# Queries and keys of three retention heads by seven products of halves instead of eight, with a larger ring for accumulating DMAs

## The chip, the cores and the metric

The kernel runs on one core of a Trainium2 chip. The metric is the device time of one execution in microseconds (us). Each value of a run is the time of one execution; the median of several is compared.

## The reference

Two residual layers over x of 512 tokens by 1024 features, then a final RMS norm. The first layer (latent attention and pooling) is not touched by the change, except for where one of its tiles lives. The second is a retention layer with 4 heads, 256 query and key features and 512 value features per head:

```python
h = rms_norm(x, norm_g)
proj = h @ w_in                                   # 1024 -> 1024 q | 1024 k | 2048 v | 2048 gate
q, k, v, gate = jnp.split(proj, [RET_QK, 2 * RET_QK, 2 * RET_QK + RET_V], axis=-1)
q = apply_rope(q.reshape(B_, T, 4, 256), cos_r, sin_r)
k = apply_rope(k.reshape(B_, T, 4, 256), cos_r, sin_r) * 256 ** -0.5
# o = sum of a forward and a backward retention: scores q k^T times a decay by distance, times v
...
o = (o - mean(o)) * rsqrt(var(o) + eps) * gn_g    # per head
y = (o * silu(gate)) @ w_out
return x + y
```

where `rope` rotates the first 128 features of a head against the second 128: (x1 cos - x2 sin, x2 cos + x1 sin).

## The kernel before

All arithmetic is float32 carried as a pair of fast-mode numbers: `split` writes a high part by a cast on ScalarE (ACT) and the rest by a subtraction on VectorE (DVE). A product of two such pairs is three matmuls on TensorE (PE): high by high, high by low, low by high (`mm3`). A weight tile of 128 x 1024 goes the same way: it is loaded into a buffer `raw` (4 of them) by a DMA from SyncE's queue (SP), then cast to `wH` (4) and subtracted into `wL` (3). Sums stand in PSUM banks of 128 x 512: four called `mm`, two `sc`, two `tr`.

The code is written in one order; a scheduler that knows the program's dependencies sets the order in which each engine's instructions stand, and the engines keep that order. So an instruction that waits holds back everything behind it on its own engine. `pin` keeps an instruction at its place in the written order relative to the others so marked.

The second layer works through the heads one after the other. For head h the stages are:

1. Queries and keys. `qk_gemm` goes through four column blocks of 128 (two of q, two of k), each 8 input blocks times three matmuls over all 512 tokens, and `rope_pair` rotates the results on DVE and splits them. In between PE does the last turn (four transposes) of the head before (`then=pend[2]`).
2. `r_out`: the output projection of the head before, from its turned results `ys`. Its weights are scaled while they are split (`out_weights`). It is written behind the queries and keys so that PE has work while DVE rotates.
3. `r_scores`: keys by queries, scaled and multiplied by the decay on DVE, then split.
4. `vg`: values and gate together by seven products of halves (the 2 x 2 scheme with 7 multiplications): tokens in two halves, input features in even and odd blocks, columns in values and gate. Operand sums of the tokens' side stand ready in `forms`; sums of the weights' side come as a load on SP and an accumulating DMA from GpSimd (POOL) into a tile `tw` or `raw`. The products are called A11, S1, S4, S2, S3, A12 and A22 and go to the sums X, Y and Z. `tt` (two `tw` tiles) is the weight sum that is changed twice on DVE by adding a loaded tile.
5. `r_head_out`: scores by values for each block t of 128 tokens, the product with the gate (DVE, line 871), its squares (ACT, line 872), and the turn of block t - 1 (line 863) after block t's matmuls.

[...] The norm's power -0.5 is a POOL instruction (line 175).

Of the kernel before, what the change touches and what calls it, by code (L numbers as in the profile page):

```python
# [12 lines left out]
F32R = mybir.dt.float32r  # L13
# [3 lines left out]
ALU = mybir.AluOpType  # L17
AX = mybir.AxisListType

P = 128  # L20
T = 512
# [16 lines left out]
def trunk(ctx: ExitStack, tc: tile.TileContext, x, positions, a_norm_g, a_w_in, a_q_norm_g, a_w_uq,  # L38
          a_kv_norm_g, a_w_ukv, a_pool_w, a_pool_scale, a_w_out, r_norm_g, r_w_in, r_decay_fwd,
          r_decay_bwd, r_gn_g, r_w_out, final_norm_g, freqs, edges, out):  # L40
    nc = tc.nc
# [21 lines left out]
    V = nc.vector  # L63
# [4 lines left out]
    def f(ap):  # L68
        return ap.bitcast(F32)
# [53 lines left out]
    lg = C("lg", (P, 8))  # L123
    nlb = C("nlb", (P, 8))
    fsum = C("fsum", (P, 16))
    r2, nr2, r2s = [C(n, (P, 8))[:, 0:4] for n in ("r2", "nr2", "r2s")]
    C("fill", (P, 16))
    w_in = a_w_in[0]
    vrow0 = S("t")[:8, :P]
    nc.scalar.dma_start(vrow0, a_norm_g.rearrange("o (k p) -> (o k) p", p=P))  # L130
# [193 lines left out]
            act(junk[:, 0:256], xt[t][q], AF.Square, accum_out=ssq[:, 4 * t + q:4 * t + q + 1])  # L324
    ss = S("sm", (P, 4))
    V.tensor_reduce(out=ss, in_=ssq.rearrange("p (t q) -> p t q", q=4), axis=AX.X, op=ALU.add)
    R = C("R", (P, T))
    rp = bcast(pow_mhalf(ss, 1.0 / DM))
    nc.scalar.copy(R, rp)

# [334 lines left out]
    def load(tag, first, *more, then=lambda i: i):  # L665
        raw = S(tag, (P, 1024))
        v = raw.rearrange("p (a b) -> p a b", a=2)
        nc.sync.dma_start(v, first)
        for one in more:
            then(G.dma_start(v, one, accum_op=ALU.add))  # L670
# [70 lines left out]
    def qk_gemm(c0, n=2, then=None):  # L741
        pts = []

        def ev(m, pt):
            pts.append(pt)
            if then and m == 0:
                then()

        gemm_T(wr, c0, n, ev, hH, hL)
        return pts  # L750

    def rope_pair(pts, tag):
# [5 lines left out]
        V.tensor_sub(a, a, b)  # L758
        V.tensor_add(c, c, d)
        return split(a, tag), split(c, tag)  # L760

    def vg(h, tt=None):

        tags = dict(X=("mm", "mm"), Z=("mm", "tr"), Y=("mm", "sc"))
# [35 lines left out]

        b11 = [load("raw", src(0, 0, i)) for i in rng]
        if tt is None:
            tt = first_sums(h)
        product("A11", "X", b11, True)
        p1 = [S("t") for _ in rng]
        for p in rng:
# [32 lines left out]
            gs[2 + p] = c  # L839
        return vv, gs  # L840

    def r_scores(q, k, ds, tag):
        ss = []
        for j in range(4):
            tk = slice(j * P, (j + 1) * P)
            pt = PS("sc")
            for i in range(2):
                mm3(pt, k[i][0][:, tk], k[i][1][:, tk], q[i][0], q[i][1], i == 0, i == 1)
            s = S("t")
            V.scalar_tensor_tensor(out=s, in0=pt, scalar=r2s[:, j:j + 1], in1=ds[j], op0=ALU.mult, op1=ALU.mult)  # L850
            ss.append(split(s, tag))
        return ss

# [99 lines left out]
    for h in range(4):  # L953
        A, B = ("qk", "y") if h % 2 == 0 else ("y", "qk")
        if h == 0:
            res = [residual(0), residual(1)]
            next(res[0])
            pq = qk_gemm(0, 1)
            sums_of_halves(0)
            sums_of_halves(1)  # L960
            next(res[0])
            pq += qk_gemm(P, 1)
            pk = qk_gemm(1024, 1)
            sums_of_halves(2)
            sums_of_halves(3)
            next(res[1])
            next(res[1])
        else:
            pq = qk_gemm(h * 256, then=pend[2])
            pk = qk_gemm(1024 + h * 256, 1)  # L970
            rs = out_scale(pend[1])
        q = rope_pair(pq, A)
        k = rope_pair(pk + qk_gemm(1024 + h * 256 + P, 1), A)
        if h == 0:
            V.tensor_add(ss2[:, 0:4], ss2[:, 0:4], ss2[:, 4:8])
            V.tensor_copy(r2, pow_mhalf(ss2[:, 0:4], 1.0 / DM))
# [56 lines left out]
```

## Time and profile before

| what | value |
|---|---|
| median of 3 runs | 794.5 us (793.38 to 794.87) |
| profiled execution, its time | 795.08 us |
| its span, first to last instruction | 793.3 us |
| mean granted clock of TensorE | 0.996 |
| PE busy | 780.8 us, 98% |
| DVE busy | 579.1 us, 73% |
| ACT busy | 403.6 us, 51% |
| POOL busy | 39.1 us, 5% |
| moved by DMA | 80.91 MB |

Busy times are of the profiled execution, and shares are of its span. Matmuls overlap their neighbours, so a matmul's duration is longer than the distance at which matmuls follow one another. Idle time of an engine is put down to the one whose signal ended it. A line such as L871 is a line of the kernel's file; `tw<-...` names the tile that is written, without its number.

### The profile page before, as it was taken

Reading aid. Unit: us, or ns where it says so; the run is one execution under the profiler, and the core shown is the slowest. Engines: PE = TensorE matmul, PEld = TensorE weight load, DVE = VectorE, ACT = ScalarE, POOL = GpSimd, SP = SyncE. Lnnn points to the kernel's source line nnn. Section 1 sums busy time; section 2 is a strip of 40 time slices with the busy share of each in tenths; the row PEclk is TensorE's granted clock in tenths of the full one; section 3 lists DMA queues with packets and bytes.
Section 4 is the critical chain, followed back from the end, with each engine's and each line's share of the span. In section 5 each row is a group of like instructions: output and inputs, shape, how many; then the busy total and the mean of one; then the engine's idle time right before and its main releaser. Section 6 shows DMA issues by size and latency. Waiting matters only on the chain.

```text
span 793.3 us, 9592 instructions
## 1 busy us (share of the span) xinstructions
PE 780.8 (98%) x3546; PEld 642.3 (81%) x3546; DVE 579.1 (73%) x935; ACT 403.6 (51%) x671; POOL 39.1 (5%) x61
## 2 busy tenths in 40 slices
PE   8999999999999999999999999999999999999996
PEld 6888888888888888888877888888888888888885
DVE  4689986768738777899679837788377884767845
ACT  6645346766716754317754833358333583324832
POOL 0000000000000000100010010100101001010003
PEclk9999999999999999999999999999999999999999
DMA  7722233123123312363315732447324473244202
GB/s 240 222 73 80 73 83 91 40 71 100 54 64 93 105 31 78 75 158 112 93 44 131 207 85 80 109 107 198 91 72 117 104 195 84 70 130 95 92 27 107
DMA packets 87832, 80.91 MB, mean 102 GB/s; under 512 B 7868, under 2 KB 67304, under 8 KB 87784
## 3 DMA queue, kind: packets, MB, share of 16 engines
q1 hardware_dynamic: 83128, 71.37, 29.9%
q0 software_dynamic: 4352, 8.39, 6.9%
q8 instruction: 28, 0.46, 0.3%
q10 hardware_dynamic: 304, 0.53, 0.2%
q14 instruction: 20, 0.16, 0.1%
HBM read 76.87 MB, written 2.10 MB: 100 GB/s over the span
## 4 chain that ended last, share of the span: by engine, by line
PE 84%; issue 10%; DVE 3%; POOL 1%; DMA 1%; ACT 0%; SPq 0%; POOLq 0%; DVEq 0%
PE mm L72 19%; PE mm L76 19%; PE mm L75 19%; PE mm L780 4%; PE mm L781 4%; PE mm L778 4%; PE tr L561 2%; PE sc L72 2%; PE sc L75 2%; PE sc L76 2%; PE sc L780 1%; PE sc L781 1%; PE sc L778 1%; PE sc L542 1%; PE sc L543 1%
## 5 line engine op out<-in xcount | busy, mean ns | idle before, releaser
L72 PE MATMUL mm<-hT,wH 128*128 128x512 f32 x352 | 138.8, 394 | 0.0
L75 PE MATMUL mm<-hT,wH 128*128 128x512 f32 x352 | 138.0, 392 | 0.0
L76 PE MATMUL mm<-hT,wL 128*128 128x512 f32 x352 | 137.9, 392 | 0.0
L108 ACT CAST wH<-raw 128x1024 fp32r<-128x1024 f32 (+3 forms) x85 | 74.3, 884 | 114.3 <-PE mm L75 91.2
L109 DVE TENSOR_TENSOR wL<-raw,wH 128x1024 fp32r<-128x1024 f32 (+3 forms) x85 | 85.6, 1012 | 13.1 <-issue 4.7
L76 PEld LDWEIGHTS mm<-hT,wL 128*128 128x128 f32 x352 | 66.5, 189 | 13.9
L75 PEld LDWEIGHTS mm<-hT,wH 128*128 128x128 f32 x352 | 66.5, 189 | 13.6
L72 PEld LDWEIGHTS mm<-hT,wH 128*128 128x128 f32 x352 | 66.6, 189 | 13.4
L770 ACT CAST wH<-raw 128x1024 fp32r<-128x1024 f32 x32 | 33.7, 1054 | 50.1 <-PE mm L76 20.2
L771 DVE TENSOR_TENSOR wL<-raw,wH 128x1024 fp32r<-128x1024 f32 x32 | 38.9, 1222 | 10.3 <-issue 7.1
L770 ACT CAST wH<-tw 128x1024 fp32r<-128x1024 f32 x24 | 25.1, 1047 | 41.0 <-PE mm L76 26.3
L890 ACT ACTIVATE wH<-raw,cols 128x512 fp32r<-128x512 f32 x32 | 21.4, 717 | 44.1 <-issue 33.1
L911 DVE SCALAR_TENSOR_TENSOR xT<-mm,sm,xT 128x512 f32<-128x512 f32 (+1 forms) x33 | 24.2, 733 | 25.1 <-PE mm L76 25.0
L75 PE MATMUL mm<-y,wH 128*128 128x512 f32 x96 | 37.2, 390 | 0.0
L76 PE MATMUL mm<-y,wL 128*128 128x512 f32 x96 | 37.2, 389 | 0.0
L72 PE MATMUL mm<-y,wH 128*128 128x512 f32 x96 | 37.2, 391 | 0.0
L771 DVE TENSOR_TENSOR wL<-tw,wH 128x1024 fp32r<-128x1024 f32 x24 | 29.3, 1222 | 2.8 <-PE tr L780 1.0
L781 PE MATMUL mm<-wH,hT 128*128 128x512 f32 x80 | 31.1, 389 | 0.0
L780 PE MATMUL mm<-wL,hT 128*128 128x512 f32 x80 | 31.1, 389 | 0.0
L778 PE MATMUL mm<-wH,hT 128*128 128x512 f32 x80 | 31.0, 389 | 0.0
L871 DVE TENSOR_TENSOR l<-mm,l 128x512 f32<-128x512 f32 x16 | 11.1, 692 | 23.8 <-PE mm L76 23.8
L490 DVE TENSOR_TENSOR xT<-mm,xT 128x512 f32<-128x512 f32 x24 | 16.5, 690 | 15.0 <-PE mm L76 14.8
(355 smaller groups left out, 1896.5 us busy)
## 6 DMA issues: line engine op xcount, KB each, us to landing
raw<-in_r_w_in_dram SPq DMA_DIRECT2D x48, 512.0 KB, 3.7
raw<-in_a_w_in_dram SPq DMA_DIRECT2D x25, 512.0 KB, 4.0
raw<-in_a_w_out_dram SPq DMA_DIRECT2D x16, 512.0 KB, 3.9
raw<-in_r_w_out_dram SPq DMA_DIRECT2D x16, 512.0 KB, 5.5
tw<-in_r_w_in_dram SPq DMA_DIRECT2D x8, 512.0 KB, 3.9
tw<-in_r_w_in_dram POOLq DMA_DIRECT2D x8, 512.0 KB, 6.9
raw<-in_r_w_in_dram POOLq DMA_DIRECT2D x8, 512.0 KB, 6.2
l<-in_x_dram SPq DMA_DIRECT2D x8, 256.0 KB, 5.7
```

Source lines behind the costliest of these rows:

```text
L72: i = mm(pt, lhsT=lH, rhs=rH, start=st, stop=False)
L75: mm(pt, lhsT=lH, rhs=rL, start=False, stop=False)
L76: mm(pt, lhsT=lL, rhs=rH, start=False, stop=sp)
L108: then(nc.scalar.copy(h[:, c], raw[:, c]))
L109: then(V.tensor_sub(l[:, c], raw[:, c], f(h[:, c])))
L770: nc.scalar.copy(wh, ws[i])
L771: V.tensor_sub(wl, ws[i], f(wh))
L778: mm(o, lhsT=lh, rhs=wh[:, c], start=first and i == 0 and k2 == 0, stop=False, skip_group_check=True)
L780: mm(o, lhsT=lh, rhs=wl[:, c], start=False, stop=False, skip_group_check=True)
L781: mm(o, lhsT=ll, rhs=wh[:, c], start=False, stop=last and k2 == 1, skip_group_check=True)
L890: act(wh[:, c], raw[:, c], AF.Copy, scale=g)
L911: V.scalar_tensor_tensor(out=a, in0=pt[:, :T // n], scalar=rs[:, t:t + 1], in1=a, op0=ALU.mult, op1=ALU.add)
```

## The change

For heads 1 to 3 stage 1 becomes `qk_halves`, the same scheme of seven products as in `vg`, with q's and k's columns as the two column halves. One product has the weights as the fixed side (128 x 128 each) and a half of the tokens, 256 columns, as the moving side: two column blocks times four input blocks times three matmuls. X, Y and Z take three of the four `mm` banks. The results come out as halves of tokens (k of the first half, k of the second, q of the first, q of the second), so each rotation is done by halves, and high and low parts are written by halves. In this scheme one of the two has the wrong sign, and `r_scores` of these heads multiplies with `nr2s` instead of `r2s`. The first weight sum (`tq`, a tile `tw`) is loaded and accumulated behind `vg` of the head before; `t3` is loaded into a `raw` tile and accumulated within the stage. The ring for accumulating DMAs is 2048 instead of 1024. The norm tile R of the first layer takes a buffer of `x2`, which the second layer uses later for operand forms.

```diff
-    r2, nr2, r2s = [C(n, (P, 8))[:, 0:4] for n in ("r2", "nr2", "r2s")]
-    C("fill", (P, 16))
+    r2, nr2, r2s, nr2s = [C(n, (P, 8))[:, 0:4] for n in ("r2", "nr2", "r2s", "nr2s")]
+    C("fill", (P, 8))
...
-    R = C("R", (P, T))
+    R = S("x2")
...
+    def qk_load(tag, h, *srcs):
+        raw = S(tag, (P, 1024))
+        v = raw.rearrange("p (a b) -> p a b", a=4)
+        for i, (r, c) in enumerate(srcs):
+            one = wv[:, r, :, c * 1024 + h * 256:c * 1024 + (h + 1) * 256]
+            if i:
+                pin(G.dma_start(v, one, accum_op=ALU.add))
+            else:
+                nc.sync.dma_start(v, one)
+        return raw
+
+    def qk_halves(h, tag, tt, then):
+        ps_ = {n: PS("mm") for n in "XZY"}
...
+        def product(name, a, w, first):
+            wh, wl = S("wH", (P, 1024), F32R), S("wL", (P, 1024), F32R)
+            nc.scalar.copy(wh, w)
+            V.tensor_sub(wl, w, f(wh))
+            for u in range(2):
+                o = ps_[a][:, u * H2:(u + 1) * H2]
+                for k in range(4):
+                    c = slice(k * 256 + u * P, k * 256 + (u + 1) * P)
+                    rh, rl = forms[k][name]
+                    mm(o, lhsT=wh[:, c], rhs=rh, start=first and u == 0 and k == 0, stop=False,
+                       skip_group_check=True)
+                    mm(o, lhsT=wh[:, c], rhs=rl, start=False, stop=False, skip_group_check=True)
+                    mm(o, lhsT=wl[:, c], rhs=rh, start=False, stop=k == 3, skip_group_check=True)
...
+        def rope(n, half, c):
+            ts = slice(half * H2, (half + 1) * H2)
+            v = c.rearrange("p (u t) -> p u t", u=2)
+            m1, m2 = S("t"), S("t")
+            for m, tab in ((m1, cosr), (m2, sinr)):
+                V.tensor_mul(m.rearrange("p (u t) -> p u t", u=2), v,
+                             tab[:, ts].unsqueeze(1).to_broadcast([P, 2, H2]))
+            o = S("t")
+            V.tensor_sub(o[:, :H2], m1[:, :H2], m2[:, H2:])
+            V.tensor_add(o[:, H2:], m2[:, :H2], m1[:, H2:])
+            for u in range(2):
+                hh, ll = outs[n][u]
+                us = slice(u * H2, (u + 1) * H2)
+                nc.scalar.copy(hh[:, ts], o[:, us])
+                V.tensor_sub(ll[:, ts], o[:, us], f(hh[:, ts]))
+
+        b11 = load("raw", (0, 0))
+        product("A11", "X", b11, True)
+        p1 = S("t")
+        nc.scalar.copy(p1, X)
+        then()
+        b22 = load("raw", (1, 1))
+        product("S1", "Z", tt, True)
+        v = S("t")
+        V.tensor_add(v, Z, p1)
+        t3 = load("raw", (0, 1), (1, 1))
+        V.tensor_add(tt, tt, b22)
+        product("S4", "Z", b22, False)
+        b21 = load("raw", (1, 0))
+        product("S2", "Y", tt, True)
+        u2 = S("t")
+        V.tensor_add(u2, Y, p1)
+        V.tensor_add(u2, Z, u2)
+        rope("k", 0, u2)
+        V.tensor_add(tt, tt, b21)
+        product("S3", "Y", t3, False)
+        V.tensor_add(v, Y, v)
+        rope("k", 1, v)
+        product("A12", "X", b21, False)
+        rope("q", 0, X)
+        product("A22", "Y", tt, False)
+        V.tensor_add(p1, Y, p1)
+        rope("q", 1, p1)
+        return outs["q"], outs["k"]
...
         else:
-            pq = qk_gemm(h * 256, then=pend[2])
-            pk = qk_gemm(1024 + h * 256, 1)
             rs = out_scale(pend[1])
-        q = rope_pair(pq, A)
-        k = rope_pair(pk + qk_gemm(1024 + h * 256 + P, 1), A)
+            q, k = qk_halves(h, A, tq, pend[2])
...
+            V.tensor_scalar(out=nr2s, in0=r2, scalar1=-0.0625, scalar2=1.0, op0=ALU.mult, op1=ALU.mult)
...
-        ss = r_scores(q, k, decay(h), B)
+        ss = r_scores(q, k, decay(h), B, r2s if h == 0 else nr2s)
         vv, gs = vg(h, tt0 if h == 0 else None)
+        if h < 3:
+            tq = qk_load("tw", h + 1, (0, 0), (0, 1))
         pend = r_head_out(ss, vv, gs, A)
...
-    nc = _bacc.Bacc("TRN2", target_bir_lowering=False, num_devices=1, dynamic_dma_scratch_size=1024)
+    nc = _bacc.Bacc("TRN2", target_bir_lowering=False, num_devices=1, dynamic_dma_scratch_size=2048)
```

`load` in `qk_halves` is `qk_load` with the head filled in. The order of the instructions moves at three places. Rows of the changed kernel bear its own line numbers: its L784 is the split of a weight tile in `qk_halves`, L919 and L953 are L837 and L871 of before (gate's evacuation, product with the gate), L973 is L891 of before.

The first place is DVE at the end of `vg` and the begin of `r_head_out` (here of head 0). Before:

```order
L109 TENSOR_TENSOR wL_4317<-raw_4314,wH_4316 128x1024
L793 SCALAR_TENSOR_TENSOR V_4145<-t_3999,sm_4141,V_4144 128x512
L109 TENSOR_TENSOR wL_4357<-raw_4354,wH_4356 128x1024
L837 TENSOR_TENSOR l_992_4216<-mm_3920,t_3958 128x512
L109 TENSOR_TENSOR wL_4388<-raw_4385,wH_4387 128x1024
L837 TENSOR_TENSOR l_993_4219<-sc_3921,t_3959 128x512
L871 TENSOR_TENSOR l_986_4180<-mm_4223,l_986_4180 128x512
```

The same place on DVE now:

```order
L784 TENSOR_TENSOR wL_4338<-raw_4335,wH_4337 128x1024
L875 SCALAR_TENSOR_TENSOR V_4147<-t_4001,sm_4143,V_4146 128x512
L784 TENSOR_TENSOR wL_4379<-tw_4224,wH_4378 128x1024
L919 TENSOR_TENSOR l_993_4218<-mm_3922,t_3960 128x512
L919 TENSOR_TENSOR l_994_4221<-sc_3923,t_3961 128x512
L825 TENSOR_TENSOR tw_4224<-tw_4224,raw_4376 128x1024
L784 TENSOR_TENSOR wL_4413<-raw_4376,wH_4412 128x1024
L953 TENSOR_TENSOR l_987_4182<-mm_4228,l_987_4182 128x512
```

The second weight split there now reads the accumulated tile `tw`, and the sum `tw += b22` and the split of `b22` stand ahead of the first product with the gate.

The second place is POOL in the same stretch. Before:

```order
L670 DMA tw_4697<-in_r_w_in_dram 128x2x512
L670 DMA tw_4700<-in_r_w_in_dram 128x2x512
L175 TENSOR_TENSOR sm_4418<-sm_4416,mhalf 128x4
L670 DMA raw_4779<-in_r_w_in_dram 128x2x512
L670 DMA raw_4782<-in_r_w_in_dram 128x2x512
```

POOL now:

```order
L768 DMA tw_4224<-in_r_w_in_dram 128x4x256
L175 TENSOR_TENSOR sm_4321<-sm_4319,mhalf 128x4
L768 DMA raw_4408<-in_r_w_in_dram 128x4x256
L670 DMA tw_4813<-in_r_w_in_dram 128x2x512
L670 DMA tw_4816<-in_r_w_in_dram 128x2x512
```

The accumulations of the seven products for q and k stand on both sides of the norm's power, and those for the gate stage come behind them.

The third place is the passage from queries and keys to the output projection (`r_out`). On DVE before, the first weight split of the projection (L891) stands right behind the first rotation's sums:

```order
L757 TENSOR_TENSOR t_4424<-mm_4360,l_755_3175 128x512
L758 TENSOR_TENSOR t_4421<-t_4421,t_4422 128x512
L759 TENSOR_TENSOR t_4423<-t_4423,t_4424 128x512
L891 SCALAR_TENSOR_TENSOR wL_4491<-raw_4488,cols,wH_4490 128x512
L82 TENSOR_TENSOR y_4432<-t_4421,y_4431 128x512
```

On DVE now (the last 12 of the rows from S3's evacuation to that split):

```order
L813 TENSOR_TENSOR y_4334<-t_4518,y_4333 128x256
L804 TENSOR_TENSOR t_4554<-mm_4324,l_757_3177 128x512
L840 TENSOR_TENSOR t_4365<-mm_4326,t_4365 128x512
L807 TENSOR_TENSOR t_4557<-t_4553,t_4554 128x256
L808 TENSOR_TENSOR t_4557<-t_4554,t_4553 128x256
L804 TENSOR_TENSOR t_4593<-t_4365,l_756_3176 128x512
L813 TENSOR_TENSOR y_4328<-t_4557,y_4327 128x256
L804 TENSOR_TENSOR t_4594<-t_4365,l_757_3177 128x512
L813 TENSOR_TENSOR y_4330<-t_4557,y_4329 128x256
L807 TENSOR_TENSOR t_4597<-t_4593,t_4594 128x256
L808 TENSOR_TENSOR t_4597<-t_4594,t_4593 128x256
L973 SCALAR_TENSOR_TENSOR wL_4607<-raw_4604,cols,wH_4606 128x512
```

The split of the projection's weights has moved behind all four rotations. On PE before, at the same passage, the matmuls of one bank follow one another:

```order
L76 MATMUL mm_4445<-hT_3544,wL_4442 128x512
L72 MATMUL mm_4504<-wH_4490,qk_4260 128x512
L75 MATMUL mm_4504<-wL_4491,qk_4260 128x512
L76 MATMUL mm_4504<-wH_4490,qk_4261 128x512
L72 MATMUL mm_4504<-wH_4490,qk_4260 128x512
L75 MATMUL mm_4504<-wL_4491,qk_4260 128x512
```

On PE now:

```order
L793 MATMUL mm_4326<-hT_3545,wL_4565 128x256
L72 MATMUL mm_4620<-wH_4606,qk_4265 128x512
L72 MATMUL mm_4634<-wH_4606,qk_4290 128x512
L72 MATMUL mm_4648<-wH_4606,qk_4315 128x512
L72 MATMUL mm_4662<-wH_4606,qk_4372 128x512
L72 MATMUL sc_4751<-y_4327,y_4331 128x512
L72 MATMUL sc_4764<-y_4327,y_4331 128x512
L75 MATMUL mm_4620<-wL_4607,qk_4265 128x512
```

The first high-part matmuls of four banks and of two score tiles have moved ahead of the first matmul that needs the low part `wL`; the two score tiles read the rotated q and k.

More of the change, by code (lines that the diff above doesn't have):

```diff
@@ L760, in rope_pair, with load @@
         return split(a, tag), split(c, tag)
+    def qk_load(tag, h, *srcs):
[10 more added lines that the diff above has]
+        ps_ = {n: PS("mm") for n in "XZY"}
+        def load(tag, *srcs):
+            return qk_load(tag, h, *srcs)
+        def product(name, a, w, first):
[11 more added lines that the diff above has]
+                    mm(o, lhsT=wl[:, c], rhs=rh, start=False, stop=k == 3, skip_group_check=True)
+        X, Y, Z = (ps_[n] for n in "XYZ")
+        outs = {n: [(S(tag, dt=F32R), S(tag, dt=F32R)) for _ in range(2)] for n in "qk"}
+        def rope(n, half, c):
[41 more added lines that the diff above has]
+        return outs["q"], outs["k"]
@@ L802, in vg @@
         if tt is None:
-            tt = first_sums(h)
+            tt = first_sums(h, pin)
         product("A11", "X", b11, True)
@@ L840, in vg, with r_scores @@
         return vv, gs
-    def r_scores(q, k, ds, tag):
+    def r_scores(q, k, ds, tag, rs):
         ss = []
@@ L849, in r_scores @@
             s = S("t")
-            V.scalar_tensor_tensor(out=s, in0=pt, scalar=r2s[:, j:j + 1], in1=ds[j], op0=ALU.mult, op1=ALU.mult)
+            V.scalar_tensor_tensor(out=s, in0=pt, scalar=rs[:, j:j + 1], in1=ds[j], op0=ALU.mult, op1=ALU.mult)
             ss.append(split(s, tag))
@@ L967, in trunk @@
             next(res[1])
-        else:
-            pq = qk_gemm(h * 256, then=pend[2])
-            pk = qk_gemm(1024 + h * 256, 1)
+            q = rope_pair(pq, A)
+            k = rope_pair(pk + qk_gemm(1024 + P, 1), A)
+        else:
             rs = out_scale(pend[1])
-        q = rope_pair(pq, A)
-        k = rope_pair(pk + qk_gemm(1024 + h * 256 + P, 1), A)
+            q, k = qk_halves(h, A, tq, pend[2])
         if h == 0:
```

## The prediction

> **What bounds the kernel now.** I read the page's busy times first, then the stretches of the second layer, then single instructions on each engine around the place of the change.
>
> ```profile
> span 793.3 us, 9592 instructions
> PE 780.8 (98%) x3546; PEld 642.3 (81%) x3546; DVE 579.1 (73%) x935; ACT 403.6 (51%) x671; POOL 39.1 (5%) x61
> PE 84%; issue 10%; DVE 3%; POOL 1%; DMA 1%; ACT 0%; SPq 0%; POOLq 0%; DVEq 0%
> ```
>
> The tensor engine is busy 98% of the span and makes 84% of the chain that ended last. By stretches, heads 1 and 2 of the second layer (100 us each) leave it no idle time at all, while the vector engine (DVE) has work for 69 us of 100:
>
> ```profile
> 510.00:610.00 100.00, 100.00 (x450) 82.72 (x449) 69.39 (x93) 46.48 (x67) 5.92 (x5) 1.00 0.44 117
> 610.00:710.00 100.00, 100.00 (x450) 82.67 (x450) 69.38 (x94) 46.47 (x67) 5.94 (x5) 1.00 0.44 117
> ```
>
> Columns: stretch, its length, then busy time of PE, weight loads, DVE, ACT, POOL; granted clock; DMA share; GB/s. So fewer PE cycles shorten the span, provided nothing else becomes late. There is no PE idle time in which a late DVE result could hide: each microsecond that PE waits is added.
>
> A matmul's duration (0.39) overlaps its neighbours, so what it costs is the distance between starts. The last rows of the program have both widths back to back:
>
> ```profile
> 779.05 0.39 PE L72 MATMUL mm<-wH,y 128*128 128x512 f32 x1
> 783.59 0.39 PE L76 MATMUL mm<-wH,y 128*128 128x512 f32 x1
> 783.81 0.28 PE L72 MATMUL mm<-wH,y 128*128 128x256 f32 x1
> 783.82 0.19 PEld L75 LDWEIGHTS mm<-wL,y 128*128 128x128 f32 x1
> 786.08 0.28 PE L75 MATMUL mm<-wL,y 128*128 128x256 f32 x1
> ```
>
> Twenty steps of 512 columns take 4.54 us, 0.227 each; nineteen of 256 take 2.27 us, 0.1195 each. A weight load lasts 0.19 but does not hold the 256-wide ones to 0.19.
>
> **The change, part by part.** Times below are on the clock of the passage from head 1 to head 2 in the trace of before; the changed stage stands in heads 1, 2 and 3, so each term counts three times.
>
> *Products.* Four blocks of 24 matmuls of 512 columns (96 x 0.227 = 21.8 us) become seven of 24 matmuls of 256 (168 x 0.1195 = 20.1 us): -1.7 us a head. [...]
>
> *The first operand sum (`tw`).* Product S1 needs even rows of q's weights plus even rows of k's: a load on SP, then an accumulating DMA from POOL. The buffer is free only when the previous `vg` has split its last use of it. The same buffer, at the same moment, is refilled in before, but for the gate stage of the next head, far behind:
>
> ```profile
> 541.06 1.22 DVE L771 TENSOR_TENSOR wL<-tw,wH 128x1024 fp32r<-128x1024 f32 x1 [0.24 <-ACT V L792]
> 542.31 3.82 SPq L668 DMA_DIRECT2D tw<-in_r_w_in_dram  x2
> 547.11 1.21 POOL L670 DMA_DIRECT2D tw<-in_r_w_in_dram  x1 [32.48 <-DMA tw<-in_r_w_in_dram]
> tw<-in_r_w_in_dram POOLq DMA_DIRECT2D x1, 512.0 KB, 9.3
> tw<-in_r_w_in_dram POOLq DMA_DIRECT2D x1, 512.0 KB, 8.6
> tw<-in_r_w_in_dram POOLq DMA_DIRECT2D x1, 512.0 KB, 8.2
> ```
>
> The load took 4.8 us; the last three rows are this accumulation (KB, us from issue to landing) at the three passages, beside other loads. I take 8.2, since one of the loads that crowded it (the second weight block of the output projection) now comes later. Landing: 547.1 + 8.2 = 555.3. The order places the split of this tile on DVE where before a weight split from a plain load stood, ahead of everything the head's end needs; both engines run in order, so ACT (cast) and DVE (difference) stand until 555.3, and these rows stand behind them:
>
> ```profile
> 549.58 1.23 DVE L109 TENSOR_TENSOR wL<-raw,wH 128x1024 fp32r<-128x1024 f32 x1 [0.76 <-ACT wH L108]
> 550.74 0.69 DVE L837 TENSOR_TENSOR l<-mm,t 128x512 f32<-128x512 f32 x1
> 554.82 0.69 DVE L871 TENSOR_TENSOR l<-mm,l 128x512 f32<-128x512 f32 x1 [1.06 <-PE mm L76]
> 557.34 0.60 PE L863 MATMUL tr<-ident,l 128*128 128x128 f32 x4
> L770 ACT CAST wH<-tw 128x1024 fp32r<-128x1024 f32 x24 | 25.1, 1047 | 41.0 <-PE mm L76 26.3
> ```
>
> After landing come cast 1.05, difference 1.13 (step of a 1024-wide DVE row, below), two gate evacuations at 0.60, the sum `tw += b22` 1.13, another difference 1.13, and only then the product of gate and output that the turns read, 0.69: with signals 6.5 us. PE has work without them until the first turn at 557.34. Wait: 555.3 + 6.5 - 557.3 = **+4.5 us** a head. Bounds: with the fastest load (3.6) and accumulation (5.9) landing is 551.8 and the wait 1.0; with 4.8 and 9.3 it is 5.6.
>
> ```profile
> DMA to landing us min/median/max: 3.6/3.7/7.2
> DMA to landing us min/median/max: 5.9/6.2/9.3
> ```
>
> (The first row is of the loads of L668, the second of the accumulations of L670.)
>
> *The second operand sum (`t3`).* Its accumulation is pinned behind the norm's `pow` on POOL, so it starts after that, in an idle DMA system:
>
> ```profile
> 565.95 1.03 POOL L175 TENSOR_TENSOR sm<-sm,mhalf 128x4 f32<-128x4 f32 x1 [7.98 <-DVE sm L173]
> 564.10 0.48 PE L72 MATMUL mm<-hT,wH 128*128 128x512 f32 x1
> ```
>
> Issue 567.0, landing at the median 6.2: 573.2. The first block starts at 564.10. With the order of the blocks on PE (A11, turn 0.35, S1, nine of S2, S4, the rest of S2, nine of A12, S3, the rest of A12, A22) the nine of A12 begin at 575.9. Their split stands behind t3's on ACT and DVE: two casts (to 575.3) and two differences (to 576.6), against the third matmul at 576.15: **+0.45 us**. Bounds 0.15 (5.9) and 3.5 (9.3).
>
> *DVE behind the last products.* Per head DVE gains three splits, two sums of 1024 columns, five evacuating sums and finer rotations. Steps:
>
> ```profile
> 571.07 1.22 DVE L109 TENSOR_TENSOR wL<-raw,wH 128x1024 fp32r<-128x1024 f32 x1
> 572.20 0.68 DVE L82 TENSOR_TENSOR y<-tr,y 128x512 fp32r<-128x512 f32 x1
> 577.00 0.68 DVE L758 TENSOR_TENSOR t<-t,t 128x512 f32<-128x512 f32 x1
> 577.60 0.69 DVE L759 TENSOR_TENSOR t<-t,t 128x512 f32<-128x512 f32 x1
> 578.20 0.75 DVE L891 SCALAR_TENSOR_TENSOR wL<-raw,cols,wH 128x512 fp32r<-128x512 f32 x1
> L928 DVE TENSOR_TENSOR t<-xT,qk 128x256 f32<-128x256 f32 x1 | 0.4, 426 | 0.0
> ```
>
> A 1024-wide row costs 1.13, a 512-wide one 0.60. A 256-wide one lasts 0.26 less than a 512-wide one (0.426 against 0.69), so I take a step of 0.34; bounds 0.30 (half) and 0.43 (its duration). From the end of S3 to the first split of the output projection DVE has 22 rows in a line, 8 of 512 and 14 of 256: 8 x 0.60 + 14 x 0.34 = 9.6 us, then that split, 0.75. S3 ends at 580.35 (579.9 plus the 0.45), so the split is ready at 580.55 + 9.6 + 0.75 = 590.9. PE has only the rest of A12, A22 and six leading matmuls to cover it: 585.0 + 6 x 0.227 = 586.4. Wait **+4.5 us**; bounds 3.9 and 5.8. Before, the split was due much earlier on DVE (578.20) and PE never stood.
>
> *Edits at nothing.* The ring of twice the size lets two accumulations start together; before, the second of a pair waited until the first had landed:
>
> ```profile
> 413.77 1.23 POOL L670 DMA_DIRECT2D raw<-in_r_w_in_dram  x1
> 420.20 1.22 POOL L670 DMA_DIRECT2D raw<-in_r_w_in_dram  x1 [5.20 <-issue]
> ```
>
> No PE wait hangs on those pairs, since PE is full where they are used (the stretches above). The shared norm tile is used up in the first layer, long before its buffer is taken again. `nr2s` is one small DVE row. More bytes: three more 512 KB loads a head, at a DMA share of 0.44; they are early enough but for the two sums above.
>
> *Sum.* -1.7 + 4.5 + 0.45 + 4.5 = +7.75 us a head, +23.2 for three. The profiled execution took 795.1 us (span 793.3), 0.6 above the median 794.5. So 795.1 + 23.2 = 818.3 on its scale, 818 against the median.
>
> **The rivals.**
>
> *The first sum is in time.* If it lands before 550.8 it costs nothing and only the end of the stage waits: (-1.7 + 0.15 + 4.5) x 3 = +9, 804. Against it: load and accumulation would have 8.5 us, and the shortest rows make 9.5. [...]
>
> *The clock falls.* PE's waits are as long as what lowered the clock at the start, where only transposes ran from 4.4 to 9.1 us:
>
> ```profile
> 1.44 2.93 PE L157 MATMUL sc<-t 128*128 128x512 f32 x6 [1.44 <-POOL t L154]
> 9.10 0.57 PE L72 MATMUL mm<-hT,wH 128*128 128x512 f32 x1
> ...
> 8.00:10.00 2.00, 1.77 (x11) 1.34 (x10) 2.00 (x5) 1.77 (x6) 0.00 (x0) 0.83 1.04 368
> 10.00:12.00 2.00, 2.00 (x6) 1.54 (x5) 1.44 (x3) 2.00 (x7) 0.00 (x0) 0.50 1.08 390
> 12.00:14.00 2.00, 2.00 (x9) 1.62 (x8) 1.32 (x3) 1.10 (x5) 0.00 (x0) 0.81 0.98 352
> ```
>
> The granted clock lost 0.17, 0.50 and 0.19 of 2 us each: 1.7 us. Six such falls make +10, 828. [...]
>
> *DVE keeps up, and it is faster.* The gate stage already runs seven products with PE full and DVE nearly so:
>
> ```profile
> 510.00:530.00 20.00, 20.00 (x90) 16.47 (x89) 18.70 (x22) 10.95 (x13) 1.22 (x1) 1.00 0.40 106
> ```
>
> If DVE's results come no later than PE asks (at 557.3 and at 586.4), only -1.7 x 3 = -5 is left: 790. It decides at the tail: its 22 rows would have to fit into 5.9 us instead of 10.4. There a stage lasts 168 x 0.227 = 38 us and splits go ahead of the stage; here a whole rotation depends on the last block.
>
> *Weight loads bind.* If a 256-wide matmul cost a load, 0.188, the blocks take 31.6 us; the tail's wait shrinks to 1.9: (9.8 + 4.5 + 1.9) x 3 = +49, 843. The steps of 0.1195 speak against it.
>
> **How the numbers follow.** Forecast 0.62 (its own range 808 to 828), the sum in time 0.10, the clock 0.15, DVE keeping up 0.06, weight loads 0.03; 0.04 for a middle in which the waits just eat the gain. A change under 0.2% (1.6 us) cannot be told from none in this kernel. Slower: 0.62 + 0.10 + 0.15 + 0.03 and a little of the middle, 0.91; same 0.03; faster 0.06. Range: the sums of the low bounds (-1.7 + 1.0 + 0.15 + 3.9) x 3 = +10 and of the high ones (-1.7 + 5.6 + 3.5 + 5.8) x 3 = +40, the upper drawn in because the bounds will not all meet: 804 to 832.
>
> **What would show it.** Right: PE idle before the first turn of each head's end, released by DVE, with DVE waiting on the `tw` DMA; PE idle before the first low-part matmul of the output projection, DVE full there; block steps of 0.12; nothing changed before 440 us. Wrong: `tw` landing within 8.5 us of its load, or the 256-wide DVE rows at far under 0.3 us.

## The result, and the profile after

The changed kernel takes 832.2 us (median of 4; 831.03 to 835.55) against 793.9 for the kernel before in the same runs: ratio 1.0485, 95% interval 1.0463 to 1.0507. That is 38.2 us slower. 818 was forecast, with 832 as the upper end of the range.

The head of its page: span, busy times, and the chain that ended last by engine.

```profile
span 830.5 us, 10150 instructions
PE 790.7 (95%) x3762; PEld 655.9 (79%) x3762; DVE 606.0 (73%) x990; ACT 415.8 (50%) x695; POOL 46.9 (6%) x67
PE 68%; issue 17%; DVE 8%; DMA 4%; POOL 1%; ACT 1%; SPq 0%; POOLq 0%; DVEq 0%; ACTq 0%
```

PE is busy for 95% and no longer 98, and DVE, which had 3% of the chain, has 8, with 4 more for DMA. What PE waits for in the second layer (engine, sum and line; then who releases it: us in total, times, longest):

```profile
PE tr L945 <- DVE l L953: 15.4, 3, 5.5
PE sc L72 <- ACT y L812: 5.6, 2, 2.8
PE sc L72 <- ACT qk L812: 2.8, 1, 2.8
PE mm L72 <- DVE t L804: 2.3, 3, 0.8
PE mm L793 <- DVE wL L784: 0.7, 2, 0.5
```

The first row is the wait before the first turn, three times; the next three are the end of the stage (L812 is the cast of a rotated half, L804 a rotation's multiplication); the last is the second operand sum `t3`. These are the three places of the forecast; at the stage's end it had another matmul waiting. Stretches of the first head's passage (length; busy PE, weight loads, DVE, ACT, POOL; granted clock; DMA share; GB/s):

```profile
461.00:574.00 113.00, 103.95 (x520) 87.66 (x520) 77.97 (x110) 50.50 (x75) 8.52 (x7) 0.95 0.48 117
455.00:461.00 6.00, 1.02 (x5) 0.52 (x3) 5.31 (x7) 3.98 (x5) 0.00 (x0) 0.89 0.00 0
461.00:467.00 6.00, 5.97 (x18) 4.85 (x19) 1.26 (x2) 2.05 (x5) 0.00 (x0) 0.54 0.31 87
491.00:497.00 6.00, 2.37 (x12) 1.34 (x11) 6.00 (x14) 3.14 (x8) 0.35 (x1) 1.00 0.60 89
497.00:501.00 4.00, 4.00 (x11) 3.02 (x12) 4.00 (x8) 0.11 (x1) 0.00 (x0) 0.57 0.23 70
```

From one first turn to the next it is 113 us where it was 100. In 455 to 461 PE is busy for 1 us of 6, in 491 to 497 for 2.4. And in the stretch right behind each of these waits PE is busy all the time, but at a granted clock of 0.54 and 0.57. The matmuls show it, start by start:

```profile
455.63 0.39 PE L76 MATMUL mm<-V,y 128*128 128x512 f32 x1
461.03 1.11 PE L945 MATMUL tr<-ident,l 128*128 128x128 f32 x4 [5.02 <-DVE l L953]
464.08 0.63 PE L76 MATMUL mm<-V,y 128*128 128x512 f32 x1
464.50 0.63 PE L72 MATMUL mm<-V,y 128*128 128x512 f32 x1
467.74 0.40 PE L76 MATMUL mm<-V,y 128*128 128x512 f32 x1
467.98 0.39 PE L72 MATMUL mm<-V,y 128*128 128x512 f32 x1
```

Steps of 0.42 behind the wait, and of 0.24 or less again from 467.7 on. In front of it, the operand sum: the load on SP, the accumulation on POOL, then ACT's cast and DVE's difference.

```profile
441.39 0.37 SPq L770 DMA_DIRECT2D tw<-in_r_w_in_dram  x1
446.77 1.30 POOL L768 DMA_DIRECT2D tw<-in_r_w_in_dram  x1 [32.30 <-ACT l L915]
454.60 1.05 ACT L783 CAST wH<-tw 128x1024 fp32r<-128x1024 f32 x1 [6.96 <-DMA tw<-in_r_w_in_dram]
455.69 1.23 DVE L784 TENSOR_TENSOR wL<-tw,wH 128x1024 fp32r<-128x1024 f32 x1 [7.84 <-ACT wH L783]
460.29 1.28 DVE L953 TENSOR_TENSOR l<-mm,l 128x512 f32<-128x512 f32 x2
```

The cast waits 6.96 us for the DMA and DVE 7.84 for the cast, with the gate products (L953) behind them. At the stage's end these rows show the begin and the end of DVE's line from S3's end to the first split, and what PE does meanwhile:

```profile
487.00 0.69 DVE L835 TENSOR_TENSOR t<-mm,t 128x512 f32<-128x512 f32 x1 [0.29 <-PE mm L793]
496.59 0.74 DVE L973 SCALAR_TENSOR_TENSOR wL<-raw,cols,wH 128x512 fp32r<-128x512 f32 x1
491.47 0.28 PE L793 MATMUL mm<-hT,wL 128*128 128x256 f32 x1
493.01 1.00 PE L72 MATMUL mm<-wH,qk 128*128 128x512 f32 x2 [0.78 <-DVE t L804]
496.82 0.85 PE L72 MATMUL sc<-y,y 128*128 128x512 f32 x2 [2.82 <-ACT y L812]
497.48 0.70 PE L75 MATMUL mm<-wL,qk 128*128 128x512 f32 x1
```

Over the three heads it comes out like this (us a head; a wait is the distance between starts less the matmul's normal step, a clock loss is what the steps exceed 0.227 by, the turn included):

| term | forecast | measured |
|---|---|---|
| seven products instead of four blocks | -1.7 | -1.7 (reckoned from steps of 0.12) |
| wait before the first turn | +4.5 | +5.3 (5.2, 5.7, 5.0) |
| half speed behind it | none | about +2.6 |
| wait for `t3` | +0.45 | +0.3 |
| wait at the stage's end | +4.5 | +4.3 |
| half speed behind it | none | about +1.8 |
| sum | +7.75 | +12.6 |

Three times 12.6 is 37.8, against 38.2 measured. The first wait and the one at the stage's end were then taken out by runs of their own, each with the half speed behind it, and the half speed behind the first wait also by itself; the wait for `t3` was not.

### The profile page after: what moved, and what is told of

It is laid out like the page before. It is cut to its first block, busy times and chain, and to the rows that moved or that the text cites. A ratio compares the mean times of both kernels' runs of the same rounds, so it can differ in the third digit from the quotient of the medians.

```text
span 830.5 us, 10150 instructions
## 1 busy us (share of the span) xinstructions
PE 790.7 (95%) x3762; PEld 655.9 (79%) x3762; DVE 606.0 (73%) x990; ACT 415.8 (50%) x695; POOL 46.9 (6%) x67
## 4 chain that ended last, share of the span: by engine, by line
PE 68%; issue 17%; DVE 8%; DMA 4%; POOL 1%; ACT 1%; SPq 0%; POOLq 0%; DVEq 0%; ACTq 0%
PE mm L75 14%; PE mm L76 14%; PE mm L72 14%; PE mm L862 3%; PE mm L863 3%; PE mm L860 3%; DMA tw<-in_r_w_in_dram 2%; PE sc L72 2%; PE tr L561 2%; DMA raw<-in_r_w_in_dram 2%; PE sc L76 2%; PE sc L75 2%; DVE t L804 1%; PE mm L793 1%; DVE wL L853 1%
## 5 line engine op out<-in xcount | busy, mean ns | idle before, releaser
L108 ACT CAST wH<-raw 128x1024 fp32r<-128x1024 f32 (+3 forms) x73 | 62.2, 859 | 114.2 <-PE mm L75 85.3
L72 PE MATMUL mm<-hT,wH 128*128 128x512 f32 x256 | 100.2, 391 | 0.0
L75 PE MATMUL mm<-hT,wH 128*128 128x512 f32 x256 | 99.8, 390 | 0.0
L76 PE MATMUL mm<-hT,wL 128*128 128x512 f32 x256 | 99.7, 390 | 0.0
L109 DVE TENSOR_TENSOR wL<-raw,wH 128x1024 fp32r<-128x1024 f32 (+3 forms) x73 | 70.8, 976 | 8.0 <-PE mm L76 4.3
L76 PEld LDWEIGHTS mm<-hT,wL 128*128 128x128 f32 x256 | 48.1, 188 | 9.9
L75 PEld LDWEIGHTS mm<-hT,wH 128*128 128x128 f32 x256 | 48.1, 188 | 9.8
L72 PEld LDWEIGHTS mm<-hT,wH 128*128 128x128 f32 x256 | 48.1, 188 | 9.7
L852 ACT CAST wH<-tw 128x1024 fp32r<-128x1024 f32 x24 | 25.1, 1047 | 40.9 <-PE mm L76 26.3
L853 DVE TENSOR_TENSOR wL<-tw,wH 128x1024 fp32r<-128x1024 f32 x24 | 29.3, 1221 | 4.8 <-PE tr L862 2.9
L784 DVE TENSOR_TENSOR wL<-tw,wH 128x1024 fp32r<-128x1024 f32 x9 | 11.0, 1221 | 24.8 <-ACT wH L783 24.5
L72 PE MATMUL mm<-wH,qk 128*128 128x512 f32 x64 | 25.9, 410 | 1.6 <-DVE t L804 1.6
```

The lines of the kernel that those rows point to most:

```text
L72: i = mm(pt, lhsT=lH, rhs=rH, start=st, stop=False)
L75: mm(pt, lhsT=lH, rhs=rL, start=False, stop=False)
L76: mm(pt, lhsT=lL, rhs=rH, start=False, stop=sp)
L108: then(nc.scalar.copy(h[:, c], raw[:, c]))
L109: then(V.tensor_sub(l[:, c], raw[:, c], f(h[:, c])))
L852: nc.scalar.copy(wh, ws[i])
```

## The experiments

**The accumulation left out.** `tq` is loaded, not summed.

```diff
-            tq = qk_load("tw", h + 1, (0, 0), (0, 1))
+            tq = qk_load("tw", h + 1, (0, 0))
```

> The changed kernel with the first operand sum `tw` made by one plain load; the accumulating DMA behind it is left out (three times in the program), and with it q's or k's part of that operand. Theory A (the accumulation's 6 to 8 us keep ACT and DVE standing, and the idle tensor engine loses its clock afterwards): the operand lands 7 to 8 us earlier, so the tensor engine's waits before the first turn (mean 5.3 us) go, and with them the half-speed matmuls behind them (2.6 us a head): 832 - 3 x 7.9 = 808. If only the wait goes and the clock falls anyway: 832 - 3 x 5.3 = 816. Rival B (the waits come from the number of DVE rows between the split and the turn, not from the accumulation's landing): 832, or at best 829.

812.9 us, ratio 1.0219 (1.0192 to 1.0246): 19 us less than the changed kernel. No wait is left before the first turn, nor the slow stretch behind it. The time is 5 us above the forecast of theory A, and 3.8 of them are the clock at the stage's end, where the wait is the same: it is half for 6.83 us (from 489.96 on at the first head) instead of 3.41, at all three heads. The last section shows what decides between the two.

**The rotation shortened.**

```diff
-            m1, m2 = S("t"), S("t")
-            for m, tab in ((m1, cosr), (m2, sinr)):
-                V.tensor_mul(m.rearrange("p (u t) -> p u t", u=2), v,
-                             tab[:, ts].unsqueeze(1).to_broadcast([P, 2, H2]))
             o = S("t")
-            V.tensor_sub(o[:, :H2], m1[:, :H2], m2[:, H2:])
-            V.tensor_add(o[:, H2:], m2[:, :H2], m1[:, H2:])
+            V.tensor_mul(o.rearrange("p (u t) -> p u t", u=2), v,
+                         cosr[:, ts].unsqueeze(1).to_broadcast([P, 2, H2]))
```

> The changed kernel with the rotation cut to one multiplication per half of the tokens (the sine product and the two combinations are left out): per head 12 DVE rows fewer, 6 of them in the line behind S3 (about 1.2 + 4 x 0.34 = 2.6 us less there). Theory A (the DVE line behind S3 holds up the output projection by 4.3 us, and the idle gap then costs another 1.8 us in clock): the wait shrinks from 4.3 to about 1.7 us and the clock does not fall behind it, 832 - 3 x (2.6 + 1.8) = 819; as low as 814 if the whole wait goes. Rival B (DVE is not what the projection waits for, the wait is the last turn's transposes and their eviction): 832.

811.3 us, 1.0210 (1.0182 to 1.0237): 21 us less, more than expected. The wait at the end went altogether. The expectation had miscounted the line: three rotations behind S3 lose one row of 0.60 and two of 0.34 each, 3.8 us and not 2.6. The rest is that behind the first waits, which are left as they were, the clock happened to be half for 3.41, 3.41 and 6.83 us in this profile, against 6.83 three times in the changed kernel; that is 2.4 us less in all.

**Both.**

> Both edits at once: `tw` by a plain load (accumulation left out) and the rotation by one multiplication a half. Theory A (two waits and the clock behind each are all of the loss): the sum of the two single effects, 832 - 24 - 13 to 18 = 790 to 795, that is at the kernel before or 1.7 us a head under it. Rival B (something else in the seven products, such as weight loads or a bound on DVE, costs too): clearly above the kernel before, 800 or more.

791.3 us, 0.9952 (0.9931 to 0.9973). The two effects add up (19.3 + 20.9 = 40.2; both: 40.9), and what remains is under the kernel before. A whole head's passage, PE full at full clock:

```profile
455.00:554.00 99.00, 99.00 (x525) 85.24 (x524) 73.78 (x99) 50.23 (x75) 7.15 (x6) 1.00 0.49 130
```

98.5 to 98.9 us a head instead of 99.9 to 100.1: the products bring 1.1 to 1.4 of the 1.7 us that were forecast. So weight loads do not bind here (steps of 0.12), and no further loss is left in a passage with these two parts out.

**Filling the wait.** 22 independent matmuls stand in the second and third wait, not in the first.

```diff
+            if t == 1 and n:
+                busy = PS("sc")
+                for _ in range(n):
+                    mm(busy, lhsT=ones, rhs=hH[0], start=True, stop=True)
             if t:
                 turn(t - 1)
...
-        pend = r_head_out(ss, vv, gs, A)
+        pend = r_head_out(ss, vv, gs, A, 22 if h in (1, 2) else 0)
```

> The changed kernel with 22 more matmuls of 512 columns (their product is not used) between the last product of the second token block and the first turn, in the second and third of the three waits; the first wait is left as it is, as a control. They last 22 x 0.227 = 5.0 us, the waits 5.2 to 5.9. Theory A (the matmuls behind the wait run at half speed because the tensor engine stood idle for 5 us): at the second and third places the granted clock stays at 1.0 and the 512-wide steps at 0.227, at the first the clock falls as in the changed kernel; time 832 - 2 x 2.6 = 827. Rival B (the clock falls at these places for another reason, such as the total load or the burst of turns): the clock is as low as before at all three, 832 or more, up to 842 if the fillers add their own time.

826.1 us, 1.0403 (1.0374 to 1.0432): more matmuls, 6.1 us less time. The stretches behind the first wait (left empty) and around the second (filled), and the filler's row:

```profile
461.00:467.00 6.00, 6.00 (x25) 4.95 (x24) 1.93 (x3) 2.62 (x8) 0.00 (x0) 0.77 0.22 81
568.00:574.00 6.00, 5.88 (x29) 4.64 (x28) 5.89 (x7) 3.99 (x6) 0.00 (x0) 1.00 0.05 5
574.00:580.00 6.00, 6.00 (x30) 4.88 (x30) 2.08 (x3) 2.61 (x8) 0.00 (x0) 1.00 0.25 85
```

```profile
568.17 5.15 PE L958 MATMUL sc<-hT,ones 128*128 128x512 f32 x22
573.44 0.66 PE L945 MATMUL tr<-ident,l 128*128 128x128 f32 x4
574.16 0.39 PE L75 MATMUL mm<-V,qk 128*128 128x512 f32 x1
574.39 0.39 PE L76 MATMUL mm<-V,qk 128*128 128x512 f32 x1
```

The turn comes nearly as late as it did (5.5 us behind the start of the block's last product, 5.9 in the changed kernel), and behind it the clock is 1.00 and the steps are 0.23. Behind the empty wait the clock falls here too, for a shorter time (3.41 us, not 6.83). That the half speed behind the first wait comes from PE standing idle is thereby shown, at two places against a third. At the stage's end no run fills the wait; there the wait and the half speed went together in the runs with the rotation shortened and with A12 moved.

**The side edits alone**, in the kernel before: ring 2048, R in `x2`.

> The kernel before with only the two side edits: the ring of the accumulating DMAs twice as large and one norm tile in a shared buffer; the products of halves for queries and keys are not in it. Theory A (these edits cost nothing, all of the loss is in the head stages): 794.5, within 0.3% of the kernel before. Rival B (the earlier start of accumulations in the first layer or the shared buffer shifts work): a difference of more than 2 us, before 440 us of the trace.

794.5 us, 1.0002 (0.9986 to 1.0019). They cost nothing.

**Only the order.** The next runs compute everything, with the same transfers; where a product or its split moves, the load of its weights moves with it. First, with no load moved, the split of the operand sum is pinned behind the last gate product:

```diff
-            nc.scalar.copy(wh, w)
-            V.tensor_sub(wl, w, f(wh))
+            keep = pin if name == "S1" else (lambda i: i)
+            keep(nc.scalar.copy(wh, w))
+            keep(V.tensor_sub(wl, w, f(wh)))
...
-            V.tensor_mul(gs[t], pt, gs[t])
-            act(S("t"), pt, AF.Square, scale=r2[:, t:t + 1], accum_out=sq[:, t:t + 1])
+            keep = pin if t == 3 else (lambda i: i)
+            keep(V.tensor_mul(gs[t], pt, gs[t]))
+            keep(act(S("t"), pt, AF.Square, scale=r2[:, t:t + 1], accum_out=sq[:, t:t + 1]))
```

> The changed kernel with one line of order: ACT's cast and DVE's difference of the first operand sum are placed behind the last gate product of the head's end instead of ahead of the gate evacuations. The DMAs are as in the changed kernel, the accumulation lands at the same distance from its load. Theory A (the late landing hurts only because the turns' inputs stand behind it in two in-order engines): the wait before the first turn goes, with the half-speed stretch behind it; S1's split has to be ready about 9 us after the first turn, 10 us after the landing; 832 - 3 x 7.9 = 808 (812 if the clock falls for longer at the tail, as with the plain load). Rival B (the landing itself is the bound, the wait only moves from the turns to S1): 826 or more, with the tensor engine standing before S1.

824.7 us, 1.0379 (1.0344 to 1.0415), a miss. The wait before the turn is gone, but the pin holds the split behind all that is written before it, A11's copy among it, and PE now stands before S1:

```profile
PE mm L791 <- ACT wH L784: 1.7, 1, 1.7
PE mm L794 <- DVE wL L785: 0.8, 1, 0.8
PE mm L791 <- DVE t L824: 0.5, 1, 0.5
```

3 us in pieces, with 1.5 to 1.7 us of half speed behind them. So PE stands before S1, as rival B said, and the time is near its 826; but it is not the landing that binds: in this run the accumulation went out at 449.05, and with the changed kernel's 7.8 us it had landed at 456.9, 13 us before S1 started at 470.2.

Second, A12 directly behind A11:

```diff
         then()
+        b21 = load("raw", (1, 0))
+        product("A12", "X", b21, False)
+        rope("q", 0, X)
         b22 = load("raw", (1, 1))
...
-        b21 = load("raw", (1, 0))
...
-        product("A12", "X", b21, False)
-        rope("q", 0, X)
         product("A22", "Y", tt, False)
```

> The changed kernel with one product moved: A12, which needs only weights as they are and finishes the first half of q, runs directly behind A11 instead of behind S3, and q's first half is rotated there. Behind S3 the DVE line has about 6 rows fewer, and the first two splits of the output projection come before the sums of S3. Theory A (the length of the DVE line behind S3 sets the tail's wait): the tail's 4.3 us and the clock loss of 1.2 to 1.8 us behind it go, 832 - 3 x 6 = 814. Rival B (the wait moves elsewhere, since DVE has the same rows in all and A12's product now asks for two weight splits at once while the gate evacuations wait): 825 to 835.

808.0 us, 1.0174 (1.0119 to 1.0229), 24 us less: the wait at the stage's end is gone as theory A says, and the first is 3.5 us instead of 5.3, since two DVE rows stand between the split and the gate products where four did. Both together:

> Both orders at once, with the whole computation. Theory A (the two waits are matters of order, not of the amount of work): 832 - 40 = 792, as with the two parts left out (791), a little under the kernel before. Rival B (DVE is too full for seven products beside the projection's splits whatever the order): one of the two waits is still there, 800 or more.

813.4 us, 1.0242 (1.0213 to 1.0272), worse than A12 alone: ahead of S1's split stand the pin and q's early rotation, and PE waits 3.6 us for ACT's cast.

**The split in the right place.** Both first splits are written into the head's end, A11's behind block 0, the sum's pinned behind the gate product of block 2. The expectation says that no DMA is moved, but the load of A11's weights now stands behind `vg` too:

```diff
+            if ws and t in (0, 2):
+                wh, wl = S("wH", (P, 1024), F32R), S("wL", (P, 1024), F32R)
+                keep = pin if t else (lambda i: i)
+                keep(nc.scalar.copy(wh, ws[t // 2]))
+                keep(V.tensor_sub(wl, ws[t // 2], f(wh)))
+                ready.append((wh, wl))
             if t:
                 turn(t - 1)
```

> The changed kernel with the splits of the first two operands written into the head's end: A11's weights behind the first token block, the operand sum's cast and difference behind the gate product of the third block and pinned there, so that only one gate product (the fourth) stands behind them. Everything is computed, no DMA is moved. Theory A (the turns wait for the operand sum only through the order on ACT and DVE, and pinning it later than the fourth gate product was too late for S1): no wait of more than 1 us before the first turn nor before S1; 832 - 3 x 6.5 = 812, as with the plain load, since the tail is left as it is. Rival B (the landing itself is the bound and the wait only moves): the tensor engine stands 2 us or more before S1 and the time is about 825, as with the pin behind the fourth block.

819.7 us, 1.0317 (1.0291 to 1.0343). Neither the turns nor S1 wait; the first wait was order. But the splits that follow come later and S4 and the products behind it wait 2.1 us a head, in pieces of at most 0.9 us: that is most of the 7 us above the 812 expected. With A12 behind A11, and then with q's first half rotated only after S1's sum:

> The same with product A12 directly behind A11 and q's first half rotated there, so that the tail has its shorter DVE line too; everything is computed. Theory A (both waits are matters of order): 790 to 794, the sum of the operand order (-20) and of the moved A12's tail (-18 to -20). Rival B (the early rotation of q takes DVE's time just where S1's, S4's and S2's splits are due, as it did with the later pin): a wait of 2 to 4 us before S1 or S4, 800 or more.

> The same as the run with A12 directly behind A11, but q's first half is rotated after S1's sum instead of ahead of it, so that S1's and S4's splits come first on DVE. Theory A (what is left of a wait there is the early rotation): at most as long as the run before it, 788 to 793. Rival B (the rotation then falls together with the splits of S2 and S3 and lengthens the tail again): 796 or more.

804.1 (1.0130; 1.0112 to 1.0148) and 803.7 (1.0114; 1.0086 to 1.0143): rival B's times, but not at its places. In the first, PE stands 2.1 us a head before the first two matmuls of the output projection, for ACT's cast of their weights (L982), and 0.7 before S3. In the second, the two pieces are 0.8 and 1.2 us a head, and the clock falls:

```profile
478.87 0.28 PE L797 MATMUL mm<-pt,wL 128*128 128x256 f32 x1
479.89 0.73 PE L72 MATMUL mm<-wH,qk 128*128 128x512 f32 x2 [0.74 <-ACT wH L982]
481.86 0.38 PE L794 MATMUL mm<-l,wH 128*128 128x256 f32 x1 [1.24 <-DVE t L835]
```

```profile
478.00:482.00 4.00, 2.02 (x13) 1.39 (x12) 3.80 (x8) 3.31 (x7) 0.00 (x0) 1.00 0.97 295
482.00:487.00 5.00, 5.00 (x27) 4.90 (x28) 3.40 (x6) 0.54 (x1) 1.20 (x1) 0.66 0.60 206
```

S3 adds into bank Y, which DVE must read first after S2 (L835), and with A12 gone nothing stood between S2 and S3. So S2 goes ahead of S4, which then covers that read:

```diff
-        product("S4", "Z", b22, False)
         product("S2", "Y", tt, True)
         u2 = S("t")
         V.tensor_add(u2, Y, p1)
+        product("S4", "Z", b22, False)
```

> The run with the two splits in the head's end and A12 behind A11, and now product S2 ahead of S4 in the program, so that S4 stands between S2's end and S3's start on the tensor engine (S3 adds into the bank that the vector engine has to read first). Everything is computed. Theory A (what was left, 3.2 us of waits before S3 and their 1.6 to 2.4 us of half speed, is an order in which nothing covers that read): no wait over 1 us in the stage, 800 - 12 = 790, under the kernel before by the products' 1.2 to 1.7 us a head. Rival B (the DVE rows of the rotation are too many for the stage whatever the order): the wait returns before the output projection's low parts, 798 or more.

> The same with q's first half rotated after S1's sum. Theory A: as the run before it, 789 to 792. Rival B (this puts only one of the projection's splits ahead of the rotation of k): a wait of 1 to 2 us before the projection's first low part, 796 to 800.

795.1 us (1.0010; 1.0001 to 1.0020) and 792.3 us (0.9971; 0.9960 to 0.9982; one execution of the seven took 4,463 us, which no trace explains, and is not in the ratio). The first, with the early rotation, still waits about 1 us before S3, at full clock. The second has one wait left, of at most 0.5 us, at full clock:

```profile
span 791.4 us, 10144 instructions
PE 778.1 (98%) x3762; PEld 648.4 (82%) x3762; DVE 605.6 (77%) x990; ACT 414.9 (52%) x695; POOL 49.6 (6%) x67
457.00:556.00 99.00, 98.72 (x521) 84.53 (x520) 78.10 (x110) 50.25 (x75) 9.42 (x7) 1.00 0.53 133
```

```profile
PE mm L794 <- DVE t L840: 0.9, 3, 0.5
```

The same DVE work as in the changed kernel (990 rows, 606 us), the same transfers, the same products: 40 us less by the order of instructions and loads alone, and 2 us under the kernel before.

## Why the prediction was wrong

- **Direction and stages: right.** The three waits are in the stages where the text put them, and nearly in the size it gave. The first two are released by the engine that it named. At the stage's end PE stood before the two score matmuls, which the text had let run ahead, and the last signal was ACT's cast of a rotated half (L812), not DVE's split of the projection's weights; both come at the end of the same DVE line, so the size came out. The line took 487.00 to 497.33, 10.3 us, for 10.35 forecast; the 6.5 from landing to the first turn were 6.43.
- **The failed step: the clock was priced as a rival with a chance of 0.15, and not as a term of the sum.** The price was there, 1.7 us a fall and +10 for six, and all six came; they cost about 2.2 us on average, 13 us in all. The wait at the stage's end is broken by single matmuls, and the clock fell all the same: in the 3.41 us ahead of the fall PE was busy for 0.60 (first head; 0.59 at the others). The wait before the first turn came out at 5.3 us, and in the 3.41 us ahead of its falls PE was busy for 0.01 or less. And the row quoted for a fall was misread as a wait as long as these: in the 3.41 us ahead of that fall PE was busy for 1.64, and no idle piece was over 1.54 (the step is shown in the last section). So the trace of before had a fall behind far less idle time than the forecast gave each wait, and the clock belonged into the sum: 818 + 13 is 831. That the time came out beside 832, the upper end of the range, is chance: that end stood for later landings and a longer DVE line, not for the clock.
- **The first operand sum: mis-sized by 0.8 us a head,** 5.3 instead of 4.5. The load took 5.4 us (4.8 taken), the accumulation 7.8 (8.2 taken), and the load went out 14.5 us ahead of where the turn was due, 15.0 taken. For three heads 2.4 us.
- **`t3` and the tail: right,** 0.3 for 0.45 and 4.3 for 4.5. **The products: right** in their steps; without waits (both parts left out) a head gained 1.1 to 1.4 us.
- **Side edits at nothing: right,** 1.0002. With the ring of 2048 the pair of accumulations into `raw` in the first head went out together (in the changed kernel two at 411.99, 2.48 us in all), where the second had gone out 6.43 us after the first.
- The rival "DVE keeps up" at 790 asked that DVE's rows fit; the last run shows that they do, in another order. The text took the order as given, which for this change was right, but its words "DVE behind the last products" read as a matter of amount, and it is one of order.

## What to carry to other kernels

Where a forecast puts an idle stretch of some microseconds into a tensor engine that was full, add the slow matmuls behind it to the sum: in these runs 1.5 to 3.1 us for each behind which the clock fell, on top of the wait. The late transfer was paid here by what stood behind its consumer on the same engine: ACT's cast waited 6.96 us for it, DVE 7.84 for the cast, and the gate products behind them came at 460.29. Before judging a transfer, look which rows stand there and whether they can stand in front. And when a product that adds into a bank is moved, ask what now covers the read of that bank: PE waited up to 1.2 us before S3 with nothing there, up to 1.0 with S4 there, and not at all with S4 there and q's rotation later.

## What the runs showed of the hardware

The granted clock was full or half (1.00 or 0.50), and nothing between (a stretch that covers both shows a mean, such as the 0.54 above). In all fifteen traces a stretch at half clock that ends before the program does lasts 3.41 or 6.83 us, and within a trace all of them start on one grid of steps of 3.41 us. So the question in these runs is how busy PE was in such a step, and not how long a single wait was. These are the steps around the two falls of the changed kernel's first head (columns as above):

```profile
456.32:459.73 3.41, 0.00 (x0) 0.00 (x0) 3.41 (x5) 2.01 (x4) 0.00 (x0) 1.00 0.00 0
459.73:463.14 3.41, 2.11 (x7) 1.91 (x8) 2.18 (x4) 2.38 (x5) 0.00 (x0) 0.50 0.50 137
463.14:466.56 3.42, 3.42 (x9) 2.64 (x8) 0.35 (x1) 0.31 (x2) 0.00 (x0) 0.50 0.05 17
493.86:497.28 3.42, 0.60 (x3) 0.30 (x2) 3.42 (x9) 1.44 (x4) 0.00 (x0) 1.00 0.50 90
497.28:500.69 3.41, 3.41 (x10) 2.63 (x9) 3.41 (x8) 0.00 (x0) 0.00 (x0) 0.50 0.18 49
```

The clock is half in the step behind the one in which PE did little (0.00 and 0.60 us busy). It stayed half for a second step where PE still stood in part of the first (2.11 us busy), and for one step where PE was busy from its start. The next two rows are from the start of the kernel before, the last two from the run with A12 behind A11, around its third wait before the first turn:

```profile
5.92:9.33 3.41, 1.64 (x12) 1.17 (x11) 2.46 (x5) 3.17 (x7) 0.00 (x0) 1.00 1.00 328
9.33:12.75 3.42, 3.42 (x10) 2.64 (x9) 2.86 (x6) 3.42 (x12) 0.00 (x0) 0.50 1.08 390
663.49:666.90 3.41, 1.81 (x9) 1.16 (x7) 1.75 (x3) 2.60 (x3) 0.00 (x0) 1.00 0.00 1
666.90:670.31 3.41, 1.54 (x9) 1.37 (x10) 2.64 (x5) 2.29 (x5) 0.00 (x0) 1.00 0.00 0
```

In the first, idle pieces of at most 1.54 us were enough. The third wait with A12 moved is as long as the two before it, which lowered the clock (3.85 us between starts, against 3.7 and 3.7), but it falls into two steps that are each busy for about half, and the clock did not fall.

Over the fifteen traces, every step in which PE was busy for less than 0.45 of it was followed by half clock, and none in which it was busy for more than 0.53; in between both occur. A slow step was followed by full clock where PE was busy for 0.86 of it or more, and by a second slow one at 0.82 or less. From this follows an estimate: a step is at 0.45 when PE idles for 1.9 us of it, and one unbroken wait of 3.8 us or more puts that much into one of two steps wherever it lies, so it is to be priced with a fall; a shorter one, or one in pieces, falls or not by how it lies on the steps. What a fall cost was half of the time that PE was busy at half clock: 1.5 to 1.7 us for one step and 2.3 to 3.1 for two in these runs.
